# The high and low halves of the output product's inputs for jobs 1 to 4: casts and subtractions made by GpSimd instead of VectorE

## The chip, the cores and the metric

The kernel runs on one core of a Trainium2 chip. The metric is the device time of one execution in microseconds (us); runs of the same kernel are compared by their medians. The engines are TensorE (PE in the profile; PEld is its weight load), VectorE (DVE), ScalarE (ACT), GpSimd (POOL) and SyncE (SP), which only issues transfers. Each engine works through its own queue in order, and semaphores order the engines among each other.

## The reference

A decoder block over 2048 positions of width 1024, all in float32. Cut to what matters here:

```
proj = h @ w_in                                   # eight parts of 1024 columns
y_rnn  = (rg_lru(conv(x_rnn)) * silu(z_rnn)) @ w_out_rnn
o      = dilated_attention_mixture(rope(q), rope(k), v)      # 8 heads, 3 window patterns
y_attn = (o * silu(z_attn)) @ w_out_attn
merged = sigmoid(g_r + b_r) * y_rnn + sigmoid(g_a + b_a) * y_attn
out    = rms_norm(x + gate * (merged @ w_o))
```

The two products with `w_out_rnn` and `w_out_attn` are the "output products" of the title.

## The kernel before

**Arithmetic.** TensorE multiplies float32 numbers that are rounded to a shorter form (`F32R`). To keep the accuracy, every operand is split into a high half, the rounded cast, and a low half, operand minus high half. `mm3` (L153 through `mm`) makes one product of three: high by high, high by low, low by high. So each split is one cast and one subtraction. Small helpers make them: `hi_act` (L161) and `hi_dve` (L164) cast on ScalarE and on VectorE, `lo_pool` (L167) and `lo_dve` (L170) subtract on GpSimd and on VectorE.

**Stages.** First come the input projections and the recurrent branch, up to about 1340 us of the span; then attention, from about 1380 to 1880 us; then the rest of the output products, the last product with `w_o` and the norm.

**Attention.** There are 16 units of one head and one half of the sequence (`Head`), and each goes through six steps (`ORDER`), so 96 slots of some 5 us, with a delay of seven slots between the scores of a step and its weighted sums. A plan written out by hand (`at`, `run`, `enlist`) says in which slot and at which place of it each piece of work is issued: scores (tile `sc`), softmax, exchange of maxima and sums between the two patterns of keys (a small product into an `sc` tile from `sm`), softmax weights, transposes (`pT`), weighted sums (`o`), and at the end of a slot the splits and loads for later ones. The order in the program is the order on every engine (`tc.manual_schedule`). VectorE masks the scores and takes their minimum (L1485), casts and subtracts the transposed probabilities (`pth`, `ptl`), and computes the softmax weights from tiny tiles (L1651 to L1674); ScalarE takes the exponentials (L1486) and scales (L1551). GpSimd subtracts for the low halves of keys and queries (`kq`), and of values (`vh`, `wh`), reorders the queries of a unit for the window pattern (`window_queries`, L1447, two casts into tile `q`) and adds two partial results (`zt`, L1688). The first of the two `q` pairs is issued one slot before the scores that read it.

**The fill.** Between these pieces the output products run as a filler: the generator `steps` yields after every step, and `spend` takes about 2.8 steps for each slot. A job is one output product for 512 positions: eight tiles of 128 output channels, eight steps (k0 to k7) for each tile, three TensorE products a step into tile `pj`. Jobs 0 to 3 are the recurrent branch, jobs 4 to 7 the attention branch. Job 0 is prepared ahead of attention; jobs 1 to 4 begin inside it; jobs 5 and later begin at its end or behind it.

**The inputs of a job** are eight pieces of 128 channels by 512 positions, `Y[j, k]`, each split into `yh` and `yl` by `split_y` (L1764 to L1770). A piece is loaded by SyncE into one of four raw buffers `R0` to `R3` (`load_yd`), so that the loads of k4 to k7 wait for the splits of k0 to k3. `SPLIT_Y` says after which step of the fill each piece is split, counted so that 0 is the first step of the old job's last tile and 8 the first step of the new job: k0 at -3, k1 to k4 at 3, 4, 5 and 7, and k5, k6 and k7 at 10, 11 and 12. Piece k is used from step 8 + k on. There are nine buffers for each of `yh` and `yl`.

Before the change, the high halves of jobs 1 to 4 are cast by VectorE and those of the other jobs by ScalarE. Of the low halves of jobs 1 to 5, those of odd k are subtracted by VectorE and those of even k by GpSimd; job 0 gives k5 to k7 to VectorE, and the jobs after 5 give it all.

Of the kernel before, what the change touches and what calls it, by code (L numbers as in the profile page):

```python
# [24 lines left out]
NB = 4  # L25
# [66 lines left out]
def decoder_block(ctx, tc, x, c, positions, g_norm, w_mod, b_mod, w_in, b_gate, conv_w, conv_b,  # L92
                  w_a, b_a, w_x, b_x, lam, w_out_rnn, w_out_attn, w_o, g_final, cst, out):
    nc = tc.nc
    cnt = [0]

    def T(pool, shape, dt, tag, **kw):
        cnt[0] += 1
        return pool.tile(shape, dt, tag=tag, name=f"{tag}_{cnt[0]}", **kw)
# [65 lines left out]

    def lo_pool(o, i, h):
        nc.gpsimd.tensor_tensor(o, i, h.bitcast(F32), ALU.subtract)  # L167

    def lo_dve(o, i, h):
        return nc.vector.tensor_tensor(o, i, h.bitcast(F32), ALU.subtract).ins  # L170
# [40 lines left out]
    def split_s(src):  # L211
        t = s_tile([P, 2, KH, P])
        hi_act(t[:, 0], src)
        lo_pool(t[:, 1], src, t[:, 0])
        return t
# [207 lines left out]
    def output_weights():  # L423

        parts = [(i, w, m, half) for i, w in enumerate((w_out_rnn, w_out_attn)) for m in range(KT) for half in range(2)]
        for x, (i, w, m, half) in enumerate(parts):
            v = {}

            def load(v=v, w=w, m=m, half=half):
                v["raw"] = raw_tile([P, KH, P])  # L430
                rows = slice(half * KH * P, (half + 1) * KH * P)
                nc.sync.dma_start(v["raw"][:], w[0, rows, m * P : (m + 1) * P].rearrange("(k p) m -> p k m", p=P))

            def split(v=v):
                v["h"] = T(wq, [P, KH, P], F32R, "s1", bufs=1)
                v["l"] = T(wq, [P, KH, P], F32R, "s2", bufs=1)
                hi_act(v["h"][:], v["raw"][:])
                lo_pool(v["l"][:], v["raw"][:], v["h"][:])

            def store(v=v, i=i, m=m, half=half):  # L440
                for l, n in enumerate("hl"):
                    nc.scalar.dma_start(wD[i, m, half, :, l], v[n][:].bitcast(F32))

            def store_raw(v=v, m=m, half=half):
                nc.scalar.dma_start(wR[m, half], v["raw"][:])

            for d, fn in ((1, load), (3, store_raw), (4, split), (5, store)) if i else ((1, load), (4, split), (5, store)):
                after_prod.setdefault(n_prod[0] + 4 * x + d, []).append(fn)
# [15 lines left out]
    def split_wv(w, k, t):  # L464
        hi_act(w[0][:, k : k + 2], t[:])
        lo_pool(w[1][:, k : k + 2], t[:], w[0][:, k : k + 2])
# [237 lines left out]
    with tc.manual_schedule():  # L704
# [87 lines left out]
        for j in range(1, 4):  # L792
            k = 2 * j
# [378 lines left out]
    for t in range(6):  # L1172
        pieces = []
        i0 = t * P
        while i0 < (t + 1) * P:
            hd, i = divmod(i0, 96)
# [547 lines left out]
    def steps(jobs):  # L1724
# [39 lines left out]
        def split_y(j, k):  # L1764
            if j < len(jobs):
                Y[j, k] = yh, yl = [T(fl, [P, CH], F32R, tag, bufs=NY) for tag in ("yh", "yl")]
                w, ys, n = jobs[j]
                t = Y0.pop((ys is yaT, n, k))
                (hi_dve if 0 < j < NB + 1 else hi_act)(yh[:], t[:])
                (lo_dve if (k % 2 if j else k > 4) or j > NB + 1 else lo_pool)(yl[:], t[:], yh[:])  # L1770

        def load_g(t):
            j, m = tiles[t]
# [21 lines left out]
        for k in range(KT):  # L1795
            split_y(0, k)
# [3 lines left out]
        for t, (j, m) in enumerate(tiles):  # L1800
            ps = T(pj, [P, CH], F32, "pj")
            for k in range(KT):
# [26 lines left out]
                yh, yl = Y[j, k]  # L1829
# [13 lines left out]
                for k1 in (LATE_SPLIT_Y if j1 > NB + 1 else SPLIT_Y).get(x, ()) if j1 else ():  # L1843
                    split_y(j1, k1)
# [371 lines left out]
```

## Time and profile before

| | us |
|---|---|
| median of 3 runs | 2173.12 |
| lowest and highest run | 2172.37, 2176.79 |
| span of the profiled execution, first to last instruction | 2175.5 |

The profiled execution has no time of its own beside its span. The page and the trace are of one execution. An engine's "busy" is the time in which an instruction of it runs; waiting isn't busy, apart from TensorE, whose products are pipelined. A stretch A:B counts us from the span's start. In the rows of a group, `yh<-R` is output and input by tile names, then partitions by elements and type, then the count, busy us and the mean ns of one; in the rows of the timeline, start, length, engine, line, operation and count, and in brackets how long the engine had been idle before and what it waited for. That releaser is inferred and can name another engine than the one that came last. The granted clock is TensorE's, as a share of full speed.

| stretch, us | TensorE idle | VectorE busy | GpSimd busy | granted clock |
|---|---|---|---|---|
| 1380 to 1445 | 0.33 | 49.97 | 40.80 | 1.00 |
| 1500 to 1540 | 0.60 | 34.90 | 26.99 | 1.00 |
| 1610 to 1660 | 4.98 | 41.61 | 31.87 | 0.97 |
| 1755 to 1800 | 3.11 | 39.33 | 27.60 | 1.00 |

These four stretches are the changes of job inside attention, from job 0 to 1, 1 to 2, 2 to 3 and 3 to 4. TensorE's idle time is the stretch less its busy time.

### The profile page before, as it was taken

To read this page: it belongs to the slowest core of one execution; us is meant where nothing else is said; L and a number is where in the kernel's file an instruction comes from. 1 tells how busy PE (TensorE), PEld (TensorE's weight loads), DVE (VectorE), ACT (ScalarE), POOL (GpSimd) and SP (SyncE) were. 2 spreads that over 40 slices of the span, in tenths; PEclk is the share of its full clock that TensorE was granted. 3 is DMA by queue.
4 is the path that set the end of the run, shared out by engine and by line. 5 is a ranking of instruction groups with operands and counts; after the bars stand their busy time and mean duration, and the time that the engine had idled before them with its cause. 6 is when DMAs were issued, how large, how long until landed. Compare 5 with 4: busy or idle time off the path is not lost.

```text
span 2175.5 us, 32647 instructions
## 1 busy us (share of the span) xinstructions
PE 2144.2 (99%) x10570; PEld 1792.5 (82%) x10571; DVE 1503.7 (69%) x2600; ACT 1296.3 (60%) x2591; POOL 1112.1 (51%) x868
## 2 busy tenths in 40 slices
PE   9999999999999999999999999999999999999998
PEld 6888788888788888888888887888888988878886
DVE  6759877868656725545446584587777787688887
ACT  5748668658644527457448532677877877444333
POOL 1467677667666323223224664466665574422444
PEclk9999999999999999999999999999999999999999
DMA  8467887886655378899996666888886777899553
GB/s 300 144 208 261 278 300 268 287 282 240 174 112 165 110 246 284 293 311 307 326 324 221 164 161 198 275 274 265 267 263 211 255 229 231 296 320 297 186 170 112
DMA packets 413040, 522.98 MB, mean 240 GB/s; under 512 B 103142, under 2 KB 278466, under 8 KB 411844
## 3 DMA queue, kind: packets, MB, share of 16 engines
q1 hardware_dynamic: 372852, 403.22, 59.6%
q10 hardware_dynamic: 34384, 99.78, 12.3%
q0 software_dynamic: 5632, 17.88, 2.6%
q8 instruction: 84, 1.38, 0.3%
q14 instruction: 88, 0.72, 0.1%
HBM read 332.02 MB, written 188.75 MB: 239 GB/s over the span
## 4 chain that ended last, share of the span: by engine, by line
PE 61%; DVE 6%; DMA 3%; ACT 2%; issue 1%; POOL 1%; SPq 0%; POOLq 0%; DVEq 0%; ACTq 0%
PE X L153 11%; PE pj L153 11%; PE V L153 11%; PE Z L153 6%; PE W L153 6%; PE Y L153 5%; PE sc L153 4%; PE o L153 4%; PE pT L1571 1%; PE pg L153 1%; PE pT L1584 1%; DVE ptl L170 1%; DVE pp L1485 1%; DVE yh L164 1%; ACT pp L1486 1%
## 5 line engine op out<-in xcount | busy, mean ns | idle before, releaser
L167 POOL TENSOR_TENSOR S<-R,S 128x512 fp32r<-128x512 f32 x192 | 296.7, 1553 | 176.9 <-ACT S L161 85.9
L153 PE MATMUL X<-T,S 128*128 128x512 f32 x1344 | 324.0, 390 | 3.1 <-ACT u L386 2.6
L153 PE MATMUL pj<-yh,S 128*128 128x512 f32 x896 | 325.8, 405 | 0.0
L153 PE MATMUL V<-T,S 128*128 128x512 f32 x1344 | 324.2, 390 | 0.2 <-DVE ev L456 0.2
L153 PEld LDWEIGHTS X<-T,S 128*128 128x128 f32 x1344 | 251.6, 188 | 58.0 <-ACT u L386 4.3
L153 PEld LDWEIGHTS V<-T,S 128*128 128x128 f32 x1344 | 251.9, 188 | 53.9 <-DVE ev L456 0.8
L167 POOL TENSOR_TENSOR S<-s,S 128x512 fp32r<-128x512 f32 x116 | 170.5, 1470 | 145.7 <-ACT S L161 109.4
L153 PEld LDWEIGHTS pj<-yh,S 128*128 128x128 f32 x896 | 169.5, 189 | 30.2 <-DVE S L170 0.7
L153 PE MATMUL pj<-yl,S 128*128 128x512 f32 x448 | 176.6, 394 | 0.3 <-POOL yl L167 0.3
L1486 ACT ACTIVATE pp<-pp,st 128x256 f32<-128x256 f32 (+3 forms) x256 | 133.6, 523 | 69.4 <-DVE st L1485 68.1
L161 ACT ACTIVATE S<-s 128x512 fp32r<-128x512 f32 x124 | 77.4, 624 | 146.9 <-DVE s L286 91.8
L153 PE MATMUL Z<-T,S 128*128 128x512 f32 x672 | 161.9, 390 | 0.0
L153 PE MATMUL Y<-T,S 128*128 128x512 f32 x672 | 161.8, 390 | 0.0
L153 PE MATMUL W<-T,S 128*128 128x512 f32 x672 | 161.6, 389 | 0.0
L161 ACT ACTIVATE S<-R 128x512 fp32r<-128x512 f32 x200 | 121.4, 622 | 59.8 <-DMA R<-in_w_in_dram 15.4
L170 DVE TENSOR_TENSOR ptl<-pT,pth 128x384 fp32r<-128x384 f32 (+1 forms) x160 | 97.9, 628 | 76.1 <-ACT pth L161 73.9
L153 PEld LDWEIGHTS W<-T,S 128*128 128x128 f32 x672 | 126.0, 188 | 26.9 <-issue 0.9
L153 PEld LDWEIGHTS Y<-T,S 128*128 128x128 f32 x672 | 125.9, 188 | 26.1
L153 PEld LDWEIGHTS Z<-T,S 128*128 128x128 f32 x672 | 125.9, 188 | 26.0
L975 DVE SCALAR_TENSOR_TENSOR xc<-xr,par,xc 128x512 f32<-128x512 f32 x96 | 102.5, 1068 | 56.7 <-ACT xc L969 54.4
L167 POOL TENSOR_TENSOR s<-R,s 128x512 fp32r<-128x512 f32 x32 | 43.5, 1360 | 191.0 <-ACT s L161 171.4
L1551 ACT ACTIVATE pp<-pp,M 128x256 f32<-128x256 f32 (+3 forms) x256 | 118.0, 522 | 9.9 <-DVE M L1674 9.9
(424 smaller groups left out, 4949.0 us busy)
## 6 DMA issues: line engine op xcount, KB each, us to landing
sD<-S ACTq DMA_DIRECT2D x140, 512.0 KB, 3.7
S<-sD SPq DMA_DIRECT2D x140, 512.0 KB, 5.2
S<-wD SPq DMA_DIRECT2D x82, 512.0 KB, 5.5
R<-in_w_in_dram SPq DMA_DIRECT2D x144, 256.0 KB, 3.6
wD<-s ACTq DMA_DIRECT2D x64, 256.0 KB, 4.9
kraw<-kqT SPq DMA_DIRECT2D x32, 384.0 KB, 5.5
T<-in_w_mod_dram SPq DMA_DIRECT2D x16, 512.0 KB, 8.9
vN<-ev SPq DMA_DIRECT2D x32, 256.0 KB, 2.5
```

The lines of the kernel that those rows point to most:

```text
L153: nc.tensor.matmul(o, lhsT=l, rhs=r, start=st, stop=sp, **kw)
L161: nc.scalar.activation(o, i, AF.Copy)
L164: nc.vector.tensor_copy(o, i)
L167: nc.gpsimd.tensor_tensor(o, i, h.bitcast(F32), ALU.subtract)
L170: return nc.vector.tensor_tensor(o, i, h.bitcast(F32), ALU.subtract).ins
L975: nc.vector.scalar_tensor_tensor(xc, xr[:, i : i + CH], cw(i), xc, ALU.mult, ALU.add)
L1485: nc.vector.tensor_tensor_reduce(pdst, s_ps, mask, 1.0, 3e38, ALU.add, ALU.min, m_)
L1486: nc.scalar.activation(pdst, pdst, AF.Exp, bias=m_, scale=-1.0, accum_out=l_)
L1551: nc.scalar.activation(pp, pp, AF.Copy, scale=w)
L1571: nc.tensor.transpose(pt[:, c0 + j * P : c0 + (j + 1) * P], pp[i][:, k * P : (k + 1) * P], ident)
L1584: nc.tensor.transpose(pt[:, c * P : (c + 1) * P], pp[:, half * P : (half + 1) * P], ident)
```

## The change

A new helper casts on GpSimd. For jobs 1 to 4, `split_y` lets GpSimd make all high halves, which VectorE made, and all low halves, of which VectorE made those of odd k. So each piece of these jobs has its cast and its subtraction on GpSimd, one behind the other, at the same places of the program's order. Job 0, job 5 (VectorE keeps the low halves of odd k) and the later jobs stay as they were.

```diff
+    def hi_pool(o, i):
+        nc.gpsimd.tensor_copy(o, i)
...
                 t = Y0.pop((ys is yaT, n, k))
-                (hi_dve if 0 < j < NB + 1 else hi_act)(yh[:], t[:])
-                (lo_dve if (k % 2 if j else k > 4) or j > NB + 1 else lo_pool)(yl[:], t[:], yh[:])
+                (hi_pool if 0 < j < NB + 1 else hi_act)(yh[:], t[:])
+                (lo_dve if j > NB + 1 or j > NB and k % 2 or not j and k > 4 else lo_pool)(yl[:], t[:], yh[:])
```

`NB` is 4, so `0 < j < NB + 1` is jobs 1 to 4.

## The prediction

> **What bounds the kernel now.** I read the page's head first, then the busy time by stretch of the stage that the change touches, then who waited for whom there, then the chain of waits, and last the timeline of GpSimd (POOL), VectorE (DVE) and TensorE (PE) around each change of job.
>
> ```profile
> span 2175.5 us, 32647 instructions
> ...
> PE 2144.2 (99%) x10570; PEld 1792.5 (82%) x10571; DVE 1503.7 (69%) x2600; ACT 1296.3 (60%) x2591; POOL 1112.1 (51%) x868
> ```
>
> TensorE is busy for 2144.2 of 2175.5 us, so the change can win only what TensorE idles, or runs at a lower clock, because of the splits. The span is 2.4 us above the median of the runs (2173.12), inside their spread (2172.37 to 2176.79); no other time of the profiled execution is given. I sum on the span and carry the difference over to the median.
>
> The splits that move belong to jobs 1 to 4. Their eight pieces, k0 to k7, are made around four changes of job: k0 early, k1 to k4 near the end of the old job, k5 to k7 in the new one. The busy time by stretch (columns: stretch, its length, then PE, PEld, DVE, ACT, POOL busy, granted clock, DMA) for those four places:
>
> ```profile
> 1380.00:1445.00 65.00, 64.67 (x422) 57.43 (x422) 49.97 (x162) 48.98 (x161) 40.80 (x43) 1.00 0.88 274
> ...
> 1500.00:1540.00 40.00, 39.40 (x261) 34.41 (x260) 34.90 (x95) 29.38 (x95) 26.99 (x25) 1.00 0.89 270
> ...
> 1610.00:1660.00 50.00, 45.02 (x285) 39.76 (x284) 41.61 (x98) 36.83 (x95) 31.87 (x24) 0.97 0.77 235
> ...
> 1755.00:1800.00 45.00, 41.89 (x278) 37.35 (x277) 39.33 (x91) 33.65 (x88) 27.60 (x21) 1.00 0.78 250
> ```
>
> TensorE idles 0.33, 0.60, 4.98 and 3.11 us in them. The third also runs at a mean clock of 0.97, which over 50 us is worth 1.5 us. So the first two changes of job have next to nothing to give, and the last two hold 9.6 us, 0.44% of the time. Who waited in the third (waiter, releaser, us, times, longest):
>
> ```profile
> PE sc L153 <- DVE st L1485: 2.0, 1, 2.0
> PE pT L1571 <- ACT pp L1551: 1.6, 2, 1.4
> ```
>
> and two pieces of the chain that ended last, in the same place:
>
> ```profile
> 1622.46 2.61 DVE yh L164 x2
> 1625.09 2.22 DVE yl L170
> ```
>
> TensorE waits for the softmax work of VectorE, and VectorE is late because of these very splits: 4.8 us without a pause for two casts and a subtraction.
>
> **What moves, and its price.** Four jobs of eight pieces: 32 casts leave VectorE for GpSimd, and of the 32 subtractions the 16 of odd k (the even ones are GpSimd's already). Groups by line and shape, first VectorE, then GpSimd:
>
> ```profile
> L164 DVE CAST yh<-R 128x512 fp32r<-128x512 f32 x32 | 23.3, 734 | 0.0
> ...
> L170 DVE TENSOR_TENSOR yl<-R,yh 128x512 fp32r<-128x512 f32 x18 | 21.0, 1170 | 0.5
> ```
> ```profile
> L1447 POOL CAST q<-kq 128x512 fp32r<-128x512 f32 x60 | 37.0, 646 | 0.0
> L167 POOL TENSOR_TENSOR yl<-R,yh 128x512 fp32r<-128x512 f32 x23 | 30.5, 1333 | 29.4 <-ACT yh L161 12.9 <-DVE yh L164 8.8 <-DMA kraw<-kqT 2.9
> ```
>
> VectorE gives up 23.3 us of casts and 16 x 1.17 = 18.7 us of subtractions, 42 us. No cast of this very tile on GpSimd stands in the trace; the nearest row is the cast of the queries, the same 128x512 with a reordered output. A pair of these takes 1.16 us where nothing disturbs it (below), so I take 0.60 for one, between the 0.42 of VectorE's own undisturbed cast and the group's mean of 0.65. How fast GpSimd issues, and what a subtraction pays for waiting on its own engine's cast, shown on VectorE:
>
> ```profile
> 1421.96 1.29 POOL L167 TENSOR_TENSOR yl<-R,yh 128x512 fp32r<-128x512 f32 x1
> 1423.20 1.30 POOL L1688 TENSOR_TENSOR zt<-zt,yw 128x512 f32<-128x512 f32 x1
> ```
> ```profile
> 1413.52 0.42 DVE L164 CAST yh<-R 128x512 fp32r<-128x512 f32 x1
> 1413.97 0.69 DVE L170 TENSOR_TENSOR yl<-R,yh 128x512 fp32r<-128x512 f32 x1
> ```
>
> The next instruction starts 1.24 us after a subtraction, and the hand-over from cast to subtraction is 0.03. A whole piece on GpSimd costs 0.60 + 0.03 + 1.24 = 1.87 us, and a piece whose subtraction was there already adds 0.60. Over all: 16 x 1.87 + 16 x 0.60 = 39.5 us more on GpSimd. That engine is only half busy, but it works in order, and the queue of each change of job also holds the splits of keys (kq), the reordered queries (q) and the values (vh, wh) that attention needs soon. So the sum is not one of busy times; it is whether GpSimd has pauses enough between a change's first piece and the next thing that TensorE wants from it. Every piece is queued in GpSimd's order at the place that VectorE's order shows now.
>
> The undisturbed prices, 0.69 on VectorE and 1.29 on GpSimd, are a ratio of 1.9, and by them VectorE would give up only 16 x 0.69 + 32 x 0.42 = 24 us for those 39.5. The Trainium skill (GPSIMD Engine Reference, Engine selection) says just this and speaks against the change: GpSimd takes about twice VectorE's time for elementwise work on two inputs, and only a one-input operation runs at about line rate. The trace agrees for instructions that run alone. The rows' means, 1.17 and 0.73 us on VectorE with GpSimd running beside it, make the trade even.
>
> **First change of job.** GpSimd's pauses (in brackets) and the first product of k7 on TensorE:
>
> ```profile
> 1414.36 0.91 POOL L167 TENSOR_TENSOR vh<-vraw,vh 128x256 fp32r<-128x256 f32 x1 [2.04 <-ACT vh L161]
> ...
> 1416.38 1.34 POOL L167 TENSOR_TENSOR yl<-R,yh 128x512 fp32r<-128x512 f32 x1 [1.11 <-PE pT L1571]
> ...
> 1426.72 1.30 POOL L167 TENSOR_TENSOR yl<-R,yh 128x512 fp32r<-128x512 f32 x1 [1.53 <-PE o L153]
> ```
> ```profile
> 1429.44 0.47 PE L153 MATMUL pj<-yh,S 128*128 128x512 f32 x1
> ```
>
> The low half of k6 is done at 1428.02 now. Before it come, new, k1, k3 and k5 whole (5.61) and three casts (1.80): 7.41 us, against 4.68 us of pauses. So k6 is ready at 1430.75 and k7, whole behind it, at 1432.6. TensorE wants k7's low half with its second product, 0.22 after 1429.44 (as between two products at the third change, below): 2.9 us late. GpSimd's own instructions get somewhat shorter when VectorE no longer works beside them: a pair of query casts takes 1.82 and 1.63 us at the last two changes and 1.16 at the second (below); I take 0.5 off for each change of job. Loss: 2.4 us, and no clock beside it, since the fourth stretch idles 3.11 us at a clock of 1.00.
>
> **Second.** Here the queries of the next head stand behind k1 to k3:
>
> ```profile
> 1515.19 1.30 POOL L167 TENSOR_TENSOR yl<-R,yh 128x512 fp32r<-128x512 f32 x1 [1.49 <-DVE yh L164]
> ...
> 1519.02 1.16 POOL L1447 CAST q<-kq 128x512 fp32r<-128x512 f32 x2
> ```
> ```profile
> 1519.81 1.88 PE L153 MATMUL sc<-kq,q 128*128 128x128 f32 x12
> ```
>
> New before q: 1.87 + 0.60 + 1.87 = 4.34 us, against 1.49 of pause and the 0.5. The pair ends at 1520.18 + 2.35 = 1522.5 and its first half, which TensorE wants at 1519.81, at 1521.9: 2.1 us late. k7, behind three more such pieces, may add a few tenths. Loss: 2.3 us.
>
> **Third.**
>
> ```profile
> 1632.07 1.29 POOL L167 TENSOR_TENSOR yl<-R,yh 128x512 fp32r<-128x512 f32 x1 [0.57 <-DVE yh L164]
> ...
> 1636.06 1.28 POOL L167 TENSOR_TENSOR vh<-vraw,vh 128x512 fp32r<-128x512 f32 x1 [2.70 <-DMA vraw<-vN]
> ...
> 1639.09 1.82 POOL L1447 CAST q<-kq 128x512 fp32r<-128x512 f32 x2
> ```
> ```profile
> 1640.78 1.66 PE L153 MATMUL sc<-kq,q 128*128 128x256 f32 x12
> ...
> 1650.69 0.39 PE L153 MATMUL pj<-yh,S 128*128 128x512 f32 x1
> 1650.91 0.39 PE L153 MATMUL pj<-yl,S 128*128 128x512 f32 x1
> ```
>
> k1 falls into a pause ahead of this; new before q are k2's cast, k3 and k4's cast, 3.07 us, against 3.27 of pauses and 0.5 of easing. The pair ends 0.7 earlier, at 1640.2, its first half at 1639.6. TensorE, free of the 3.4 us of waits ahead of 1640.78 (4.98 less the 1.6 of the waits' second row), would be there at 1637.4 and waits for q instead: 1.2 us won of 3.4. Behind q, TensorE takes 9.91 us now until k7's product at 1650.69, of which the 1.6 of waiting and the 1.5 of clock should go; but k5 and k6 now come 1.87 and 3.74 us after q, which makes it wait some 1.1 (estimate from 1.87 per piece against three products of 0.22 for a piece and the attention work between). Gain: 1.2 + 3.1 - 1.1 = 3.2 us.
>
> **Fourth.**
>
> ```profile
> 1760.10 1.29 POOL L167 TENSOR_TENSOR yl<-R,yh 128x512 fp32r<-128x512 f32 x1 [2.86 <-DMA kraw<-kqT]
> ...
> 1763.87 1.58 POOL L167 TENSOR_TENSOR wh<-vraw,wh 128x640 fp32r<-128x640 f32 x1 [2.48 <-ACT wh L161]
> ...
> 1775.80 1.27 POOL L167 TENSOR_TENSOR yl<-R,yh 128x512 fp32r<-128x512 f32 x1 [2.03 <-DVE yh L164]
> ...
> 1780.25 1.63 POOL L1447 CAST q<-kq 128x512 fp32r<-128x512 f32 x2
> ```
> ```profile
> 1758.07 0.93 PE L1571 MATMUL pT<-cs,pp 128*128 128x128 f32 x7
> 1758.75 0.47 PE L153 MATMUL pj<-yh,S 128*128 128x512 f32 x1
> ...
> 1783.23 0.40 PE L153 MATMUL pj<-yh,S 128*128 128x512 f32 x1
> ...
> 1785.41 0.48 PE L153 MATMUL pj<-yh,S 128*128 128x512 f32 x1
> ```
>
> All of k1 to k6 stands before q: 7.41 us against 7.37 of pauses and 0.5. So q comes only 0.5 us earlier, and TensorE's wait of 2 us for the softmax becomes a wait for q. What goes for good is the lateness of the softmax weights between the last two rows: 2.18 us where three products (0.66) and a group of transposes (0.68, the first two rows) take 1.34. k7, 1.87 behind q, gives some 0.3 of it back. Gain: 0.5 + 0.8 - 0.3 = 1.0 us.
>
> **Sum.** +2.4 + 2.3 - 3.2 - 1.0 = +0.5 us: 2176.0 as a span, 2173.6 as a median. The input loads wait for the splits to free their buffers in SyncE's queue, with loads of values, keys and weights behind them; k3's end moves by under 2 us, which these loads, used a step or more later, should hide. If not, it is part of the slow rival.
>
> **Rivals.**
> *VectorE's relief counts in full, GpSimd is never late.* It needs pieces near 1.5 us, or waits at q that the loads and ScalarE, running earlier too, pull forward. For it: ScalarE's wh and vh, for which GpSimd pauses, themselves follow VectorE's late softmax. Against it: q is already within tenths of being late at the second change. It gives -9.6 us at most, 2163.5; half of it, -5 us, 2168.
> *GpSimd becomes the bound.* If the 2.70 and 2.48 us pauses, which wait for a load and for ScalarE, stay, q comes that much later at the last two changes: the third then wins 0.5 and the fourth loses 1.5. With pieces of 2.1 us (0.65 and 1.33, the groups' means, and 0.1 of hand-over) the first two lose 1.0 and 0.6 more. Together 3.4 + 2.9 - 0.5 + 1.5 = +7.3, 2180.4. It decides when both pauses stay, or one of them with pieces of 1.95 us (0.1 us a piece is worth some 1.5 over the four). This is also the outcome that the skill's rule above would have.
> *The change does nothing of the kind* can hardly be: 32 casts of this line stand in the trace, 4 x 8, all in jobs 1 to 4.
>
> **Numbers.** Within 0.2% (4.3 us, about what a measurement of this kernel can tell from no change) lies my forecast and its near neighbours: 0.53. Faster by more needs the first rival at half its size: 0.25. Slower by more needs the second: 0.22. Terms of the sum are uncertain by 1 to 2 us each; the range is 2167.0 to 2179.5, and the likeliest case alone 2170 to 2177.
>
> **What would show it.** Right: no yh or yl of jobs 1 to 4 on VectorE; its busy time about 42 us less, GpSimd's about 40 more, a piece near 1.87 us; TensorE's waits for the softmax in the third and fourth change gone, and waits for q and yl by GpSimd of about 2 us in the first two, where there were none. Wrong: TensorE idle under 1 us in all four (first rival), or over 3 us in the last two, put down to GpSimd (second).

## The result, and the profile after

The changed kernel takes 2181.42 us (median of 7 runs, 2178.64 to 2183.79), the kernel before 2173.16 us beside it (7 runs, 2172.37 to 2177.61). The medians lie 8.3 us apart; the ratio estimated from the runs is 1.0028, with a 95% interval of 1.0019 to 1.0037: 6.1 us slower, between 4.1 and 8.0. By the ratio the time is 2179.2 us on the median from which the prediction started. The forecast was 2173.6, no change within 0.2%: the time lies just under the top of its range, 2179.5, and most of its interval on the slower side of the 0.2%, to which the prediction gave 0.22. The plain medians, 8.3 us apart, lie a little outside the interval; by them the time would be 2181.4 us, above the range.

The profiled execution of the changed kernel took 2183.79 us, 1.8 us more than its span. In its code `hi_pool` is L170 and every line behind it stands 3 lower (`lo_dve` L173, the query casts L1450, the softmax L1488, `pp` L1554). The head of its page:

```profile
span 2182.0 us, 32651 instructions
...
PE 2145.8 (98%) x10570; PEld 1793.0 (82%) x10571; DVE 1483.4 (68%) x2552; ACT 1297.2 (59%) x2591; POOL 1144.6 (52%) x916
```

GpSimd is 32.5 us busier, VectorE only 20.3 us less busy, and TensorE does the same work (2145.8 against 2144.2). The spans differ by 6.5 us. What the new casts and all subtractions of `yl` on GpSimd look like (count, then shortest, median and longest ns):

```profile
L167 POOL TENSOR_TENSOR yl<-R,yh x39: 1269/1292/1747, 1341.6 to 1887.1; 128x512 fp32r<-128x512 f32 x39
L170 POOL CAST yh<-R x32: 601/612/631, 1403.4 to 1785.3; 128x512 fp32r<-128x512 f32 x32
```

The price of the parts was right: 0.61 and 1.29 us. The busy time by stretch, with the columns of the prediction, for the four changes of job and for two short stretches behind them:

```profile
1380.00:1445.00 65.00, 61.95 (x397) 53.81 (x395) 41.76 (x144) 46.64 (x152) 45.99 (x50) 1.00 0.85 262
1500.00:1540.00 40.00, 35.88 (x235) 31.16 (x234) 27.98 (x79) 27.94 (x93) 34.65 (x38) 1.00 0.79 253
1610.00:1660.00 50.00, 48.32 (x310) 43.08 (x309) 38.16 (x98) 38.87 (x99) 43.06 (x40) 0.97 0.75 230
1755.00:1800.00 45.00, 42.94 (x279) 38.02 (x278) 35.23 (x86) 35.40 (x90) 38.08 (x34) 1.00 0.82 246
...
1817.00:1819.00 2.00, 2.00 (x9) 1.69 (x10) 1.90 (x6) 1.64 (x5) 2.00 (x2) 0.68 0.00 0
1819.00:1822.00 3.00, 3.00 (x16) 2.71 (x15) 2.57 (x8) 1.08 (x3) 1.85 (x3) 0.64 0.91 291
```

TensorE's idle time, length less busy, was 0.33, 0.60, 4.98 and 3.11 us at the four changes; it is 3.05, 4.12, 1.68 and 2.06 us. So the first two lose and the last two win, as forecast. Whom TensorE waits for between 1340 and 1890 us (us in all, times, longest):

```profile
PE sc L153 <- POOL q L1450: 5.1, 3, 2.0
PE pj L153 <- POOL yl L167: 4.5, 7, 0.9
...
PE sc L153 <- DVE st L1488: 2.1, 2, 1.8
```

The same lines of the kernel before:

```profile
PE sc L153 <- DVE st L1485: 5.4, 4, 2.2
...
PE sc L153 <- POOL q L1447: 0.6, 2, 0.5
...
PE pj L153 <- POOL yl L167: 0.3, 1, 0.3
```

The waits for VectorE's softmax (`st`) have fallen from 5.4 to 2.1 us, and those for what GpSimd makes (`q` and `yl`) have risen from 0.9 to 9.6 us.

Both traces hold the same 10570 TensorE products in the same order, so each can be set beside itself. Where attention starts the changed execution is 1.0 us ahead: the profiled execution of before ran at a granted clock of 0.50 from 1358.87 to 1362.28 us, which cost it some 1.6 us, and the changed one did not. From there the start of the same product moves, after less before:

| place | shift from, to | part | forecast |
|---|---|---|---|
| first change of job | -1.0 to +2.9 | +3.9 | +2.4 |
| second | +2.9 to +6.7 | +3.8 | +2.3 |
| third | +6.7 to +3.2 | -3.4 | -3.2 |
| at 1748 us | +3.2 to +4.1 | +0.9 | none |
| fourth | +4.1 to +3.2 | -0.9 | -1.0 |
| 1812 to 1818 us | +3.2 to +5.6 | +2.5 | none |
| behind attention | +5.6 to +6.5 | +0.8 | none |

Of the 2.5 us at 1812 to 1818 us, 0.9 are a wait and 1.6 another such stretch at 0.50 (last section). Each of the two executions has one more of them, at the third change. So over the whole the clock cancels, and what is left of the places without a forecast is waits.

**First change.** TensorE's waits, and GpSimd's queue: a pause ahead of them, and the pieces behind the last two:

```profile
1425.33 0.50 PE L153 MATMUL pj<-yl,S 128*128 128x512 f32 x1 [0.86 <-POOL yl L167]
...
1429.19 0.50 PE L153 MATMUL pj<-yl,S 128*128 128x512 f32 x1 [0.80 <-POOL yl L167]
...
1431.09 0.50 PE L153 MATMUL pj<-yl,S 128*128 128x512 f32 x1 [0.85 <-POOL yl L167]
```
```profile
1415.15 0.75 POOL L167 TENSOR_TENSOR vh<-vraw,vh 128x256 fp32r<-128x256 f32 x1 [2.04 <-ACT vh L161]
...
1427.16 0.61 POOL L170 CAST yh<-R 128x512 fp32r<-128x512 f32 x1
1427.85 1.28 POOL L167 TENSOR_TENSOR yl<-R,yh 128x512 fp32r<-128x512 f32 x1
1429.08 0.61 POOL L170 CAST yh<-R 128x512 fp32r<-128x512 f32 x1
```

From cast to cast a piece takes 1.92 us: between the cast's end at 1427.77 and the subtraction lie 0.08 us, not 0.03. Each subtraction ends just when TensorE's product goes on (1427.85 + 1.28 = 1429.13, then 1429.19). TensorE waits for k4, k5 and k6 in turn.

The first row is the longest of the pauses that were to take up the new work, and it stayed at 2.04 us. GpSimd waits there for ScalarE's cast of `vh`, which begins at 1414.67 us, 0.8 later than before, although TensorE and GpSimd ran 1.0 us ahead until then. ScalarE in turn had waited for VectorE's softmax weights. Three of VectorE's steps on 16 columns take 0.59, 0.64 and 1.09 us instead of 0.17, 0.16 and 0.21, 1.8 us more together. The last of them, after and then before:

```profile
1412.05 1.09 DVE L1672 TENSOR_TENSOR M<-dm,xs 128x16 f32<-128x16 f32 x1 [0.29 <-ACT dm L1668]
```
```profile
1412.14 0.21 DVE L1669 TENSOR_TENSOR M<-dm,xs 128x16 f32<-128x16 f32 x1 [0.29 <-ACT dm L1665]
```

It runs until 1413.14, beside GpSimd's new subtraction for k1, which lasts from 1411.82 to 1413.12.

**The other changes.** The long waits at the second, third and fourth are all for the next head's queries, behind the splits in GpSimd's order:

```profile
1524.90 2.01 PE L153 MATMUL sc<-kq,q 128*128 128x128 f32 x12 [2.04 <-POOL q L1450]
...
1645.55 2.32 PE L153 MATMUL sc<-kq,q 128*128 128x256 f32 x12 [1.50 <-POOL q L1450]
...
1784.83 2.02 PE L153 MATMUL sc<-kq,q 128*128 128x256 f32 x12 [1.55 <-POOL q L1450]
```

**At 1748 us**, far from a change of job, k0 of job 4 is split. First VectorE and GpSimd after, then VectorE before:

```profile
1748.55 1.26 DVE L1675 TENSOR_TENSOR M<-M,t__3402_17615 128x16 f32<-128x16 f32 x1
```
```profile
1748.49 1.29 POOL L167 TENSOR_TENSOR yl<-R,yh 128x512 fp32r<-128x512 f32 x1
```
```profile
1745.25 0.17 DVE L1672 TENSOR_TENSOR M<-M,t__3402_17615 128x16 f32<-128x16 f32 x1
```

A step of the softmax weights on 16 columns, 0.17 us before, takes 1.26 us and ends with GpSimd's subtraction (at 1749.81 and 1749.78). The weights come 1.1 us later and TensorE's products behind them 0.9 us.

### The profile page after: what moved, and what is told of

It reads as the page before. It is cut to its first block, busy times and chain, and to the rows that moved or that the text cites. A ratio compares the mean times of both kernels' runs of the same rounds, so it can differ in the third digit from the quotient of the medians.

```text
span 2182.0 us, 32651 instructions
## 1 busy us (share of the span) xinstructions
PE 2145.8 (98%) x10570; PEld 1793.0 (82%) x10571; DVE 1483.4 (68%) x2552; ACT 1297.2 (59%) x2591; POOL 1144.6 (52%) x916
## 4 chain that ended last, share of the span: by engine, by line
PE 57%; DMA 5%; DVE 4%; POOL 3%; ACT 2%; issue 2%; SPq 0%; POOLq 0%; ACTq 0%; DVEq 0%
PE X L153 11%; PE V L153 11%; PE pj L153 8%; PE Z L153 6%; PE W L153 6%; PE Y L153 5%; PE sc L153 4%; PE o L153 4%; DMA fg<-gaT 1%; PE pT L1574 1%; PE pg L153 1%; PE pT L1587 1%; ACT pp L1489 1%; POOL kq L167 1%; DMA fg<-mrT 1%
## 5 line engine op out<-in xcount | busy, mean ns | idle before, releaser
L173 DVE TENSOR_TENSOR ptl<-pT,pth 128x384 fp32r<-128x384 f32 (+1 forms) x160 | 97.9, 629 | 86.0 <-ACT pth L161 83.8
L1554 ACT ACTIVATE pp<-pp,M 128x256 f32<-128x256 f32 (+3 forms) x256 | 118.0, 523 | 15.8 <-DVE M L1677 15.8
```

The source lines that it names most:

```text
L1554: nc.scalar.activation(pp, pp, AF.Copy, scale=w)
```

## Experiments

Two theories. The **queue theory**: GpSimd works in order, so its longer queue brings `q` and `yl` late at the first two changes, where TensorE waited for nothing; at the last two VectorE's relief is worth more than GpSimd's lateness. The **port theory**, the rival: VectorE and GpSimd hold each other up when both read SBUF, so the loss is spread over all four changes and goes with the amount of such work beside each other. Each kernel was timed in five rounds beside the kernel before. Microseconds are the ratio times 2175.

**1. The change in jobs 3 and 4 only.**

```diff
-(hi_pool if 0 < j < NB + 1 else hi_act)(yh[:], t[:])
+(hi_pool if 3 <= j <= 4 else hi_dve if 0 < j < NB + 1 else hi_act)(yh[:], t[:])
-(lo_dve if j > NB + 1 or j > NB and k % 2 or not j and k > 4 else lo_pool)(...)
+(lo_dve if j > NB + 1 or (k % 2 if j else k > 4) and not 3 <= j <= 4 else lo_pool)(...)
```

> The change for jobs 3 and 4 alone; jobs 1 and 2 keep VectorE's casts and odd subtractions. Queue theory (the loss comes from GpSimd's queue: q and yl come late at the first two changes of job, while the last two win because VectorE is relieved): only the two winning places are left, -3.4 and -1.0 us by the shift of TensorE's instructions between the traces, so 4.4 us faster than before. Port theory (GpSimd's denser work holds up VectorE's two-input instructions at SBUF wherever they meet, and the whole loss is of that kind): half of the extra GpSimd work, so half of the loss, some 3 us slower than before.

Ratio 0.9997 [0.9989, 1.0005], -0.7 us. In its profiled run, the fastest of its twelve (2171.4, median 2174.7) and the only one of them with a mean granted clock of 0.999 (eight have 0.998), the shift of TensorE's products falls by 3.8 us at the third change and 1.1 at the fourth and rises by 0.9 at 1748:

```profile
1610.00:1660.00 50.00, 47.81 (x314) 42.43 (x313) 37.69 (x89) 40.55 (x101) 41.88 (x36) 1.00 0.85 269
1755.00:1800.00 45.00, 42.93 (x274) 37.91 (x273) 34.59 (x78) 35.57 (x85) 36.04 (x31) 1.00 0.79 256
```

The trace has the sign of the queue theory. The timed difference cannot be told from nothing: the interval is -2.4 to +1.1 us, and neither -4.4 nor the port theory's +3 lies in it. Of the 3.8 us at the third change 1.7 are clock: the profiled execution of before ran at 0.50 from 1645.59 to 1649.00 us, run 1 at 1.00.

**2. The change in jobs 1 and 2 only** (the same edit with `1 <= j <= 2`).

> The change for jobs 1 and 2 alone. Queue theory: only the two losing places, +4.0 and +3.8 us, so 7.8 us slower than before, more than the whole change. Port theory: half of the loss, some 3 us slower.

Ratio 1.0031 [1.0019, 1.0043], +6.7 us. The shift rises by 3.8 us at the first change and 3.9 at the second. The waits of TensorE, with the softmax's back where they were in the kernel before:

```profile
PE sc L153 <- DVE st L1488: 5.4, 4, 2.2
PE pj L153 <- POOL yl L167: 3.4, 4, 0.9
PE sc L153 <- POOL q L1450: 2.5, 2, 2.0
```

The interval, 4.1 to 9.4 us, holds the queue theory's 7.8 and not the port theory's 3. The two halves add up, 6.7 - 0.7 = 6.0 us, to the whole change's 6.1. So the loss is made in jobs 1 and 2, and jobs 3 and 4 give back almost nothing. This run also shows how far one execution can be trusted: at its third change, where its code is the kernel before's, it is 1.5 us quicker than the profiled run of before. That one was a poor sample there.

**3. Only the casts on GpSimd, 4. only the subtractions of odd k.**

Against the changed kernel, first 3, then 4:

```diff
-(lo_dve if j > NB + 1 or j > NB and k % 2 or not j and k > 4 else lo_pool)(...)
+(lo_dve if (k % 2 if j else k > 4) or j > NB + 1 else lo_pool)(...)
```
```diff
-(hi_pool if 0 < j < NB + 1 else hi_act)(yh[:], t[:])
+(hi_dve if 0 < j < NB + 1 else hi_act)(yh[:], t[:])
```

> Only the 32 casts go to GpSimd; the odd subtractions stay on VectorE, which now has to wait for GpSimd's cast in front of each. Queue theory: GpSimd gets only 0.69 us a piece more, so q at the second change is late by some 0.4 us instead of 2.1; but VectorE stands still behind GpSimd's queue (two subtractions of keys, 3.7 us, lie ahead of k2 at the third and k4 at the fourth change), so the gain of the last two places is gone: 0 to 4 us slower than before. Port theory: half of GpSimd's extra work and no relief of VectorE's subtractions, some 3 us slower.

Ratio 1.0069 [1.0056, 1.0081], +15 us: both theories missed. VectorE's queue has a subtraction of odd k that now needs GpSimd's cast, and stands still behind it:

```profile
1635.70 1.73 DVE L173 TENSOR_TENSOR yl<-R,yh 128x512 fp32r<-128x512 f32 x1 [6.90 <-POOL yh L170]
```

The cast is late because GpSimd is, and for 6.9 us VectorE does no softmax. So moving half of a pair costs more than twice what moving both does.

> Only the 16 odd subtractions go to GpSimd; VectorE keeps all casts. Queue theory: 1.24 us for every other piece; q at the second change late by some 0.8 us, k7 at the first by 0.5 at most; the third and fourth change win about half of what VectorE is spared, 2 and 1 us: 1 to 2 us faster than before. Port theory: half of GpSimd's extra work, some 2 to 3 us slower.

Ratio 1.0006 [0.9998, 1.0015], +1.3 us, between the two expectations; the interval, -0.4 to +3.3 us, takes in the port theory's 2 to 3 and leaves out the queue theory's gain. Here VectorE makes the cast first; GpSimd gets 16 instructions more instead of 48.

**5 and 6. Which of GpSimd's products is late?** In 5 the first pair of `q` at the second to fourth change is cast by VectorE. In 6 the pieces are split earlier, and k5 and k6 loaded earlier for it.

```diff
+        copy = nc.vector if (self.f, self.h) == (0, 0) or (self.f, self.h, i) in ((0, 6, 0), (1, 2, 0), (1, 6, 0)) else nc.gpsimd
```
```diff
-LOAD_Y = {-12: [0], -10: [1], -8: [2], -6: [3], -2: [4], 4: [5], 5: [6], 6: [7]}
-SPLIT_Y = {-3: [0], 3: [1], 4: [2], 5: [3], 7: [4], 10: [5], 11: [6], 12: [7]}
+LOAD_Y = {-12: [0], -10: [1], -8: [2], -6: [3], -2: [4], 2: [5], 4: [6], 6: [7]}
+SPLIT_Y = {-3: [0], 1: [1], 3: [2], 5: [3], 6: [4], 8: [5], 9: [6], 11: [7]}
```

> The whole change, and beside it the three pairs of query casts that stand behind the pieces at the second, third and fourth change of job are given to VectorE. Queue theory: TensorE's 5.1 us of waits for q, of which 2.0, 1.5 and 1.55 at these places, go; the late yl stay: some 5 us faster than the whole change, 0 to 2 us slower than before. Port theory: VectorE's casts meet GpSimd's dense work and wait for it, nothing is won: 6 us slower than before, as the whole change.

Ratio 1.0083 [1.0069, 1.0097], +18 us: missed. The queries need the low half of the keys, which GpSimd's late queue also makes, so VectorE waits in its place:

```profile
1638.60 1.04 DVE L1450 CAST q<-kq 128x512 fp32r<-128x512 f32 x1 [1.00 <-ACT kq L161]
1644.46 0.80 DVE L1450 CAST q<-kq 128x512 fp32r<-128x512 f32 x1 [4.82 <-POOL kq L167]
```
```profile
PE sc L153 <- DVE st L1488: 20.1, 5, 7.5
PE pj L153 <- POOL yl L167: 3.0, 4, 0.9
```

The wait for `q` is gone and a wait of 20.1 us for the softmax behind it has come. The granted clock falls to 0.91, 0.93 and 0.89 in the second to fourth stretch.

> The whole change, with the pieces' places spread: k1 to k7 after steps 1, 3, 5, 6, 8, 9 and 11 instead of 3, 4, 5, 7, 10, 11 and 12 (and the loads of k5 to k7 after 2, 4 and 6), the same instructions on the same engines. Queue theory: TensorE's 4.5 us of waits for yl go, q at the second change is late by 0.5 instead of 2 us, but k5 now stands ahead of q at the third change and costs 1.5 there: 4 to 5 us faster than the whole change, 1 to 2 us slower than before. Port theory: GpSimd works as much as in the whole change: 6 us slower than before.

Ratio 1.0039 [1.0027, 1.0052], +8.5 us, worse than the change itself:

```profile
PE sc L153 <- POOL q L1450: 10.2, 4, 3.8
...
PE pj L153 <- POOL yl L167: 1.3, 2, 0.9
```

Against the whole change the waits for `yl` fall from 4.5 to 1.3 us and those for `q` rise from 5.1 to 10.2. That is the queue theory's signature: GpSimd's work is the same, its place in the order differs, and the lateness goes from what is now ahead to what is now behind. That the queries got so much later than expected fits their lateness in the changed kernel; what the earlier loads did beside that was not tried alone.

**7 and 8. Both of these edits, and the queries alone with the change in jobs 3 and 4.**

> Both: the pieces spread, and the three query pairs on VectorE. Queue theory: neither q nor yl is late, VectorE's relief is left: 2 to 4 us faster than before. Port theory: 6 us slower than before.

> The change for jobs 3 and 4 alone, with the query pairs of the third and fourth change on VectorE. Queue theory: the 3 us of waits for q that were left with jobs 3 and 4 alone go: 2 to 4 us faster than before. Port theory: no better than jobs 3 and 4 alone, within 1 us of before.

Ratios 1.0102 [1.0087, 1.0117] and 1.0052 [1.0039, 1.0064], +22 and +11 us. Both missed for run 5's reason: VectorE waits 17.2 and 9.6 us for GpSimd's keys.

**9 and 10. The keys too on VectorE**: the subtractions of the first two key pieces of the heads behind a change, in 9 with the whole change, in 10 with jobs 3 and 4 only and without the first head of `LATER` (`q` on GpSimd in both). The lines of these two kernels stand 6 lower than the changed kernel's from there on.

```diff
+    LATER = ((0, 6), (1, 2), (1, 6))
...
+    if c < 2 and (self.f, self.h) in LATER:
+        at(NU * (H * self.f + self.h) - 2, TAIL, lo_dve, ...)
```

> The whole change, and for the three heads whose first queries were late, the low halves of the first two key pieces are subtracted by VectorE at the end of the slot, where it waits for ScalarE anyway, instead of by GpSimd ahead of the query casts. Queue theory: GpSimd reaches q earlier by two subtractions (2 x 1.24 us at the second, 2 x 1.8 at the third and fourth change), TensorE's waits of 2.0, 1.5 and 1.55 us for q go, the late yl of the first change stay: 5 to 6 us faster than the whole change, within 1 us of before. Port theory: VectorE's six subtractions from SBUF meet GpSimd's dense work and wait for it: no faster than the whole change, 6 us slower than before.

> The change for jobs 3 and 4 alone, with the same two key subtractions of the heads at the third and fourth change on VectorE. Queue theory: the 3 us of waits for q that were left with jobs 3 and 4 alone go: 3 to 4 us faster than before. Port theory: within 1 us of before.

Ratios 1.0032 [1.0019, 1.0044] and 1.0005 [0.9996, 1.0014], +7.0 and +1.1 us. Both meet the port theory's figure. In run 9 the waits for `q` fall from 5.1 to 1.9 us: those at the third and fourth change go, as the queue theory says. The one at the second stays, 1.8 us; GpSimd begins that pair at 1524.29 us, as in the changed kernel (1524.24), because it pauses 1.3 us more for ScalarE's `vh` and its next cast and subtraction take 1.07 and 1.62 us. And the keys on VectorE are dear. Run 10's group, and its first wait of TensorE:

```profile
L173 DVE TENSOR_TENSOR kq<-kraw,kq 128x768 fp32r<-128x768 f32 x4 | 8.3, 2121 | 0.0
```
```profile
PE sc L153 <- DVE st L1494: 7.6, 4, 3.2
```

A subtraction of 768 columns takes 2.12 us there. VectorE's 512 columns took 0.69 alone, which scales to an estimate of 1.04. All four run beside instructions of GpSimd. So both theories hold a part: the queue decides what is late, and the cure costs about double where both engines work. That the port is the reason is argued from this overlap, not tried.

**11 and 12. VectorE relieved without GpSimd's casts.** In 11, jobs 3 and 4 are cast by ScalarE and all their subtractions made by GpSimd; jobs 1 and 2 stay as before. In 12, ScalarE also casts for jobs 1 and 2.

The first is 11; 12 has the second in the place of its first row:

```diff
+(hi_dve if 0 < j < 3 else hi_act)(yh[:], t[:])
+(lo_dve if j > NB + 1 or (k % 2 if j else k > 4) and not 3 <= j <= 4 else lo_pool)(...)
```
```diff
+hi_act(yh[:], t[:])
```

> For jobs 3 and 4 the casts go to ScalarE instead of GpSimd, all subtractions to GpSimd; jobs 1 and 2 as before. Queue theory: GpSimd gets four subtractions of 1.24 us a job more, about half of what the change gives it, so q is on time; VectorE is relieved in full; GpSimd now waits for ScalarE's place in the order: 1 to 3 us faster than before. Port theory: GpSimd's work is what counts, about a quarter of the whole change's extra: 1 to 2 us slower than before.

> As the run before it in jobs 3 and 4 (casts on ScalarE, all subtractions on GpSimd), and in jobs 1 and 2 the casts on ScalarE too, with the subtractions shared between VectorE and GpSimd as before the change. GpSimd's queue is the same as in that run; VectorE gives up 16 more casts at the first two changes of job. Queue theory: TensorE waits for nothing of VectorE's there, so relief is worth nothing: -1 to -3 us against the kernel before, as in that run, if ScalarE's 16 more casts of 0.62 us do not make it late. Port theory: 16 casts less beside GpSimd ease both engines everywhere: -3 to -5 us. If ScalarE comes late in the first two changes, by waits for pp of it: 0 to +3 us.

Ratios 0.9991 [0.9982, 1.0000] and 0.9996 [0.9987, 1.0006], -2.0 and -0.9 us. Run 11 falls where the queue theory put it, and is the one version with a gain that reaches the edge of what can be told: its interval is -3.9 to 0.0 us. TensorE's waits in it:

```profile
PE pT L1574 <- ACT pp L1554: 4.9, 7, 2.2
PE sc L153 <- DVE st L1488: 2.8, 3, 1.4
...
PE sc L153 <- POOL q L1450: 0.7, 2, 0.6
```

The wait for `q` is down to 0.7 us, and ScalarE's weights (`pp`) are the next to be late. In run 12, VectorE's relief at the first two changes brings nothing more, which fits TensorE's idle time of 0.33 and 0.60 us there before.

## Why the prediction was right in its range and wrong in its sum

The time lies within the range, 0.3 us under its top, and outside the likeliest case, 2170 to 2177. The range held by its width and some luck: the sum was +0.5 us against +6.1. The queues that the prediction walked through are those in which most of the time went. By the timings, the first two terms came to +6.7 us (run 2) for +4.7, and the last two to -0.7 (run 1) for -4.2, so the larger part of the miss is the gain that did not come.

- **What bounds the kernel: right.** TensorE's work is unchanged, and the loss is waits around the splits.
- **Signs and owners of the four terms: right in the traces.** The first two changes lose to GpSimd, the last two win from VectorE, and the waits are for `yl` and `q`, as it said. In the timed medians run 2 shows the loss; the gain of run 1 cannot be told from nothing.
- **First term: the pauses did not take up the work.** +2.4 was taken, +3.9 stands in the trace. Of the 4.68 us of GpSimd's pauses the longest, 2.04, stayed, because the new work itself made VectorE, and behind it ScalarE, late (result, first change). So TensorE waits from k4 on, and not only for k7. The hand-over from cast to subtraction, 0.08 us and not the 0.03 read off VectorE, makes a piece 1.92 instead of 1.87, which is little beside that. The easing of GpSimd's other instructions was larger than the 0.5 taken: 1.0 us between 1380 and 1429.
- **Second term: `q` right, what follows it too small.** +2.3 was taken, +3.8 stands in the trace. `q` cost 2.2 us, the 2.1 forecast, but the "few tenths" behind it were 1.6: TensorE waits for k5, k6 and k7 in turn.
- **Third and fourth term: right in this trace, partly by luck, and too large in the timing.** -3.4 and -0.9 against -3.2 and -1.0. The two pauses of GpSimd on which its slow rival turned are both gone: from 1629 to 1655 and from 1757 to 1789 us GpSimd has no idle time in the changed kernel, and `q` comes 1.5 us late all the same. At the third change, 1.9 us were won ahead of `q` for the 1.2 forecast. Behind it the sum had 1.5 of clock, which did not come (0.97 again), and 1.1 for late pieces, which did not come either (TensorE has no wait for `yl` there). The step that failed is to take a gain from the stalls and the clock of one profiled execution. Some 1.5 us of the stall at the third change were a peculiarity of it (run 2). Run 1's trace shows -3.8 and -1.1 at the two changes and +0.9 twice, at 1748 and behind 1800 us, in all -3.1; without those 1.5 and the 1.7 of clock nothing is left, an estimate that fits the timed -0.7.
- **Left out: what VectorE pays when GpSimd reads beside it.** It took GpSimd's easing for granted and no price the other way. The trace shows it behind the pause of 2.04 us at the first change, as 0.9 us at 1748, and as 0.9 us at 1813, where 1.6 of clock follow (last section).
- **"VectorE 42 less, GpSimd 40 more": right for what moved, not for the engines.** By their rows the moved instructions are 42.1 us less on VectorE and 39.7 more on GpSimd, but the engines' busy times changed by 20.3 and 32.5. On VectorE 12 of the 22 us that came back are the steps of the softmax weights on 16 columns (last section); the rest is not taken apart here.
- **The rivals.** "GpSimd becomes the bound", +7.3 us, is next to the measured +6.1 and had pieces of 1.95 us as one of its conditions; its first two terms, 3.4 and 2.9, are the nearest to the trace. The pauses it named did not stay, so its mechanism at the last two changes is not what happened; a pause for ScalarE stayed at the first change instead. The Trainium skill's ratio of two for two-input work (GPSIMD Engine Reference, Engine selection) is what the trace shows for these instructions alone, 1.29 against 0.69, and the outcome that the prediction tied to it came.

**What stays open.** In single traces jobs 3 and 4 win about 3 us, in the median 0.7. Runs of the kernel before lie between 2171.9 and 2179.9, so one trace cannot tell which part of a 3 us gain is the usual one. From 1800 to 1885 us the shift rises by 2.5 us in the changed kernel, by 0.9 in run 1 and by nothing in run 2: whether such meetings of VectorE and GpSimd take the gain back in most executions would need many more traces.

## What to carry to other kernels

Price a move between engines at the places where the bounding engine waits, piece by piece in the receiving engine's order, and not by two sums of busy time: a half-idle engine can be full for 26 and 32 us on end, as here. A stall seen in one profiled execution is not yet a gain to be had; time the change at that place alone. Before moving a step, look at what stands behind it in that queue and who needs it; moving the lateness away from one product can give it to the next, as runs 5 and 6 show. Never leave on a busy in-order engine a step that needs the late engine's result: half a pair moved (run 3) or a cure that waits (runs 5, 7 and 8) cost two to four times the change itself.

## What the hardware showed beside that

**VectorE is held up by GpSimd even in tiny instructions.** The softmax weights work on 16 columns with both inputs in SBUF (shortest, median and longest ns, after, then before):

```profile
L1664 DVE TENSOR_TENSOR dm<-M,st x16: 175/518/1226, 1384.8 to 1853.8; 128x16 f32<-128x16 f32 x16
L1665 DVE TENSOR_TENSOR dm<-M,xs x16: 161/398/1849, 1384.9 to 1853.9; 128x16 f32<-128x16 f32 x16
...
L1677 DVE SCALAR_TENSOR_TENSOR M<-M,dm x16: 174/175/1061, 1386.3 to 1855.2; 128x16 f32<-128x16 f32 x16
```
```profile
L1661 DVE TENSOR_TENSOR dm<-M,st x16: 174/516/520, 1385.8 to 1848.2; 128x16 f32<-128x16 f32 x16
L1662 DVE TENSOR_TENSOR dm<-M,xs x16: 161/169/632, 1385.9 to 1848.3; 128x16 f32<-128x16 f32 x16
...
L1674 DVE SCALAR_TENSOR_TENSOR M<-M,dm x16: 174/175/176, 1387.4 to 1849.5; 128x16 f32<-128x16 f32 x16
```

The longest grow from 0.52, 0.63 and 0.18 us to 1.23, 1.85 and 1.06, about one GpSimd instruction each. Over attention VectorE's 128 instructions on 16 columns take 52.3 us instead of 40.3. Instructions with one input in PSUM do not grow (`ptl`, mean 691 ns for 128x512 in both). The Trainium skill (SBUF — State Buffer, Who interferes with whom) says that an instruction of VectorE with two SBUF inputs and one of GpSimd that reads SBUF exclude each other for a whole instruction, while one with at most one such input is free, unless it runs in a mode that uses both of VectorE's ports, as casts can. The trace agrees with the lock and with the free instructions, and VectorE's cast of `yh`, with its one input in SBUF, took between 0.41 and 2.07 us before the change.

**Who comes first decides, and the clock can treble the price.** The same two instructions and TensorE's wait behind them, about 1813 us before; after, then before:

```profile
1808.72 1.31 POOL L167 TENSOR_TENSOR vh<-vraw,vh 128x512 fp32r<-128x512 f32 x1
1809.00 1.58 DVE L1790 TENSOR_TENSOR fg<-fg,fg 128x512 f32<-128x512 f32 x1
...
1816.99 0.46 PE L153 MATMUL sc<-sm,msk 128*128 128x128 f32 x2 [1.84 <-DVE st L1488]
```
```profile
1805.84 0.69 DVE L1787 TENSOR_TENSOR fg<-fg,fg 128x512 f32<-128x512 f32 x1
1805.91 1.78 POOL L167 TENSOR_TENSOR vh<-vraw,vh 128x512 fp32r<-128x512 f32 x1
...
1812.95 0.46 PE L153 MATMUL sc<-sm,msk 128*128 128x128 f32 x2 [0.95 <-DVE st L1485]
```

Before, VectorE's addition starts 0.07 us ahead and GpSimd's subtraction takes 1.78 us; after, GpSimd is 0.28 us ahead and the addition takes 1.58 us for 0.69. TensorE's wait grows by 0.9 us. Then its clock falls: the two short stretches above show 0.68 and 0.64, because both take in a part of 3.41 us, from 1817.72 to 1821.13, at 0.50. That costs half of 3.41, 1.7 us more (1.6 by the shift): together the 2.5 us. The Trainium skill (TensorE: Matmul & The Clock Gate, Why this matters for your kernels) asks for no idle gap over some 3 us between bursts. Here the clock falls behind 1.84 us of idling. In run 1, behind 1.85 us of idling for the same product, it does not fall. Behind 2.04 us at 1524.90 in the changed kernel the stretch stayed at 1.00, and behind 2.03 us at the same place in run 2 it fell (0.96 over the stretch). So the length of one gap doesn't decide it in these traces, and what does was not tried.
